# Moving SBUF tiles by 64 to 192 bytes in a two-layer float32 backbone on Trainium2

## The chip, the cores and the metric

The kernel runs on one core of one Trainium2 chip. The metric is the device time of one execution, in microseconds: 3413.97 us, the median of three runs (3413.45 to 3414.4). The engines are named as the profile names them: PE (TensorE, matmuls), PEld (its weight loads), DVE (VectorE), ACT (ScalarE), POOL (GpSimd) and SP (SyncE, which here issues loads).

## What is computed

The reference runs two layers over 1,024 latent tokens of 1,024 features and 256 context tokens, in float32. Cut to its shape:

```python
for l in range(DEPTH):                              # 2 layers
    shift, scale, gate = _ada(c, w_ada[l], b_ada[l])
    h_lat = _rms(x, norm_w[l]) * (1.0 + scale) + shift
    if l % 2 == 0:   # 16 heads of neighbourhood attention || 4 heads of two-way mLSTM
        y_lat, y_ctx = _ab_mixer(h_lat, h_ctx, w_in_ab[j], ...)
    else:            # 16 heads of two-way HGRN2 (gated linear recurrence)
        y_lat, y_ctx = _c_mixer(h_lat, h_ctx, w_in_c[j], ...)
    x = x + gate * y_lat
```

Each mixer is an input projection of the normalised tokens, the heads' own work, and an output projection.

## The kernel before

**Projections.** Float32 accuracy is had from three matmuls in the faster float32r type: each operand is split into a high and a low part (`split`, lines 71 to 75; ACT casts the high part, DVE subtracts for the low one), and `dense` (lines 127 to 133) issues high x high, high x low and low x high for each block of 128 features. The profile calls these lines 130, 131 and 132; lines 861 to 863 of `out_sum` are the same trio for the output projections. In every matmul one operand is the weights loaded into the array ahead of it (128 columns), the other is streamed (the moving operand, 256 or 512 columns). Which of the two is the token tile and which the weight matrix differs: `proj_nat` streams the weight matrix (`wh`, `wl`, `wzh`, `wzl`, `wxh`) against the tokens, `proj_tr` streams the tokens (`hh`, `hl`) against the weight matrix. The profile writes the output, then the moving tile, then the weights: `mm<-wh,hh` has `wh` moving.

**Stages.** After the normalisation come layer 0's attention heads (pool `na`), its mLSTM heads (pool `ml`), its output projection (pools `oy`, `op0`, `wo1`), then layer 1's sixteen recurrent heads (pool `hg`), and its output projection. In a recurrent head, `hg_proj` projects the gates, `hg_intra` works through seven levels inside blocks of tokens with strips of 64 columns (line 1024, plain float32), `hg_vz` projects the values and the gate (weights `wz`, moving in most of its matmuls), `hg_ctx` and `hg_scan` carry the state, and `hg_out` transposes and stores.

**Order and places.** The tile framework writes out each engine's order by a simulated timeline, and sets the waits. SBUF has two sides: pools opened on the left are stacked upwards from the constants (pool `const`), pools opened on the right are stacked downwards from the top. A pool's tiles lie one behind the other in the order in which their names first come up, each name with as many buffers as it asks for. So a tile that is added moves everything that was placed behind it, also in pools stacked on top. On the right lie `hh` and `hl` (the tokens' two parts), `w1` (layer 1's weight tiles) and `oy`. On the left lies the rest: the constants, `w0` (layer 0's weight tiles), `na`, `ml`, `pre`, `gates`, `op0`, `op1`, `wo1`, `hgk` and `hg`.

The lines that the change touches: `na_qk`, line 663 (the sums of squares `ar`, three buffers); `hg_vz`, line 939; `hg_intra`, line 994; `hg_scan`, line 1115 (the sums `gss`); `build`, where the constants are loaded, line 1207 on, and where the heads are called, line 1385.

Of the kernel before, what the change touches and what calls it, by code (L numbers as in the profile page):

```python
# [10 lines left out]
F32 = mybir.dt.float32  # L11
# [8 lines left out]
P = 128  # L20
# [25 lines left out]
class Prog:  # L46
# [599 lines left out]
    def na_qk(self, p2, pool):  # L646
        nc, a = self.nc, self.a
        w = self.wring([a["wab"][:, p2 * P : (p2 + 1) * P], a["wab"][:, D + p2 * P : D + (p2 + 1) * P]], 256)
        qs = [self.t(pool, [P, T], F32R, "aqs", 4) for _ in range(2)]
        kh = [self.t(pool, [P, T], F32R, "akh", 4) for _ in range(2)]  # L650
        kl = [self.t(pool, [P, T], F32R, "akl", 4) for _ in range(2)]

        for tt in range(0, NT, 2):
            ps = self.ps("mm", [P, 2, 256])
            for j in range(2):
                self.proj_nat(ps[:, j, :], w, tt + j, 0, 256)
            raw = self.t(self.wp, [P, 2, 256], F32, "ev", 2)
            nc.scalar.copy(raw, ps)
            n = self.t(pool, [P, 2, 2, P], F32, "aqn", 2)
            g = lambda t: t.rearrange("p a b -> p (a b)").rearrange("p (a b) -> p a b", b=64)  # L660
            n8 = n.rearrange("p a b c -> p (a b c)").rearrange("p (a b) -> p a b", b=64)
            nc.scalar.activation(n8, g(raw), AF.Square)
            r = self.t(pool, [P, 8], F32, "ar", 3)
            nc.vector.tensor_reduce(r, n8, axis=AX.X, op=ALU.add)
            self.rsqrt(r, r, 1.0 / 64)
            nc.vector.tensor_tensor(out=n8, in0=g(raw), in1=r.unsqueeze(2).to_broadcast([P, 8, 64]), op=ALU.mult)

            pt = self.ps("tq", [P, 4, P])
            for i in range(4):
                nc.tensor.transpose(pt[:, i, :], n[:, i % 2, i // 2, :], self.ident)  # L670
            pq = pt[:, 0:2, :].rearrange("p a b -> p (a b)")
            pk = pt[:, 2:4, :].rearrange("p a b -> p (a b)")
            s = slice(tt * P, (tt + 2) * P)
            for hd in range(2):
                own, oth = slice(hd * 64, (hd + 1) * 64), slice((1 - hd) * 64, (2 - hd) * 64)
                if tt < LAT // P:

                    qv = qs[hd][:, (tt // 4) * 512 : (tt // 4 + 1) * 512].rearrange("p (b r c) -> p r b c", b=4, r=8)
                    qv = qv[:, 2 * (tt % 4) : 2 * (tt % 4) + 4]
                    pv = pq.rearrange("p (r b c) -> p r b c", r=4, b=4)  # L680
                else:
                    qv, pv = qs[hd][:, s], pq

                nc.scalar.copy(qv[own], pv[own])
                nc.vector.tensor_tensor(out=qv[oth], in0=pv[own], in1=qv[own].bitcast(F32), op=ALU.subtract)
                for h64 in (own, oth):
                    nc.scalar.activation(kh[hd][h64, s], pk[own], AF.Copy, scale=self.qkn[own])
                    nc.vector.scalar_tensor_tensor(
                        out=kl[hd][h64, s], in0=pk[own], scalar=self.qkn[own], in1=kh[hd][own, s].bitcast(F32),
                        op0=ALU.mult, op1=ALU.subtract,  # L690
                    )
        return qs, kh, kl
# [246 lines left out]
    def hg_vz(self, h, st, pool):  # L939
        nc, a = self.nc, self.a  # L940
        col = lambda i: a["wc"][:, i * 2048 + h * P : i * 2048 + (h + 1) * P]
        w = self.wblock(pool, "wz", [col(3), col(4)], KD, 256)
        v = self.t(pool, [P, NT, P], F32, "gv", 2)
        z = self.t(pool, [P, NT - 2, P], F32, "gz", 1)
        ps = self.ps("mm", [P, CTX])
        self.proj_tr(ps, w, 0, LAT, CTX)
        vT = self.t(pool, [P, CTX], F32, "gEc", 1)
        nc.scalar.copy(vT, ps)  # L948
        pt = self.ps("tr", [P, 2, P])
        for j in range(2):  # L950
            nc.tensor.transpose(pt[:, j, :], vT[:, j * P : (j + 1) * P], self.ident)
        nc.scalar.copy(v[:, 8:10, :], pt)
        for tt in range(0, 8, 2):

            ps = self.ps("mm", [P, 2, 256])
            for j in range(2):
                self.proj_nat(ps[:, j, :], w, tt + j, 0, 256)
            nc.scalar.copy(v[:, tt : tt + 2, :], ps[:, :, 0:P])
            sg = self.t(pool, [P, 2, P], F32, "gsg", 1)
            nc.scalar.activation(sg, ps[:, :, P:256], AF.Sigmoid)  # L960
            nc.vector.tensor_tensor(out=z[:, tt : tt + 2, :], in0=sg, in1=ps[:, :, P:256], op=ALU.mult)
        st["v"], st["z"] = v, z
# [28 lines left out]
        return S  # L991


    def hg_intra(self, st, pool):
        nc = self.nc
        F, q = st["F"], st["q"]
        K = self.t(pool, [P, 2, LAT], F32, "gK", 1)
        nc.vector.tensor_scalar(out=K, in0=F, scalar1=-1.0, scalar2=1.0, op0=ALU.mult, op1=ALU.add)
        Q = self.t(pool, [P, 2, LAT], F32, "gQ", 1)
        ks = [self.t(pool, [P, 512], F32, "gkn", 4) for _ in range(2)]  # L1000
        for hf in (1, 0):
            s = slice(hf * 512, (hf + 1) * 512)
            nc.vector.tensor_tensor(out=ks[hf], in0=K[:, 0, s], in1=K[:, 1, s], op=ALU.add)
            for d in range(2):
                nc.vector.tensor_tensor(out=Q[:, 1 - d, s], in0=q[hf], in1=F[:, d, s], op=ALU.mult)
        hv = dict(Q=Q, K=K, T=F, D=self.t(pool, [P, 8, 64], F32, "gD", 1))
        hv["A"] = self.t(pool, [P, 8, P], F32, "gA", 1)
        pa = self.ps("s", [P, 8, 64])
        with self.urgent():
            for c in range(8):  # L1010
                for b in range(2):
                    o = c % 4 * P + b * 64
                    self.strip(pa[:, c, :], b, ks[c // 4][:, o : o + 64], q[c // 4][:, o : o + 64])
        nc.vector.tensor_tensor(
            out=hv["D"], in0=pa, in1=self.lmask[:, 0, :].unsqueeze(1).to_broadcast([P, 8, 64]), op=ALU.mult
        )
        for lev in range(7):
            self.hg_level(hv, lev, pool)
        return hv
# [64 lines left out]
    def hg_scan(self, st, H, S, pool):  # L1084
# [12 lines left out]
        for c in range(8):  # L1097
            cs = slice(c * P, (c + 1) * P)
            if c % 4 == 0:
                o4 = self.ps("acc", [P, 4, P])  # L1100
            o = o4[:, c % 4, :]
            nc.tensor.matmul(o, lhsT=H["A"][:, c, :], rhs=v[:, c, :], start=True, stop=False)  # L1102
            nc.tensor.matmul(o, lhsT=H["Q"][:, 0, cs], rhs=sb[c], start=False, stop=False)  # L1103
            nc.tensor.matmul(o, lhsT=H["Q"][:, 1, cs], rhs=Sf, start=False, stop=True)
            if c < 7:
                u = self.ps("s", [P, P])
                nc.tensor.matmul(u, lhsT=H["kn"][c // 4][0][:, c % 4, :], rhs=v[:, c, :], start=True, stop=True)
                s = self.t(pool, [P, P], F32, "gS0", 2)
                nc.vector.scalar_tensor_tensor(
                    out=s, in0=Sf, scalar=H["T"][:, 0, c : c + 1], in1=u, op0=ALU.mult, op1=ALU.add  # L1110
                )
                Sf = s
            if c % 4 < 3:
                continue
            ss = self.t(pool, [P, 4], F32, "gss", 2)
            jk = self.t(pool, [P, P], F32, "gjk", 1)
            for i in range(4):
                nc.scalar.activation(jk, o4[:, i, :], AF.Square, accum_out=ss[:, i : i + 1])
            self.rsqrt(ss, ss, 1.0 / P)

            y4 = H["A"][:, c - 3 : c + 1, :]
            nc.vector.tensor_tensor(out=y4, in0=o4, in1=z[:, c - 3 : c + 1, :], op=ALU.mult)
            nc.gpsimd.tensor_tensor(out=y4, in0=y4, in1=ss.unsqueeze(2).to_broadcast([P, 4, P]), op=ALU.mult)
# [51 lines left out]
    def build(self):  # L1175
        tc, nc, a = self.tc, self.nc, self.a
        dma = nc.sync.dma_start
        with ExitStack() as es:
# [23 lines left out]
            def load(name, shape, eng=nc.gpsimd):  # L1202
                t = self.t(cp, shape, F32, name)
                eng.dma_start(out=t, in_=a[name])
                return t

            self.sc = load("cT", [P, KD, 2], nc.sync)
            self.normw = load("normw", [P, 2, KD])
            self.badap = load("badap", [P, 2, 16])
# [84 lines left out]
            with tc.tile_pool(name="ml", bufs=2) as pool, self.pp.phase(s=2, acc=2):  # L1294
# [9 lines left out]
                st, parts = self.ml_load(0, pool)  # L1304
# [72 lines left out]
            with l1:  # L1377
# [4 lines left out]
                last = None  # L1382
                st = self.hg_proj(0, pool, wf)
                for h in range(16):
                    hv = self.hg_intra(st, pool)
                    self.hg_vz(h, st, pool)
                    self.hg_close(hv, pool)
                    S = self.hg_ctx(st, pool)
# [283 lines left out]
```

## Time and profile before

| what | value |
|---|---|
| runs | 3413.97 us median, 3413.45 to 3414.4 |
| profiled execution, its own time | 3411.4 us |
| its span, first to last instruction | 3409.6 us |
| granted PE clock, mean | 0.994 |
| instructions | 64360 |
| DMA, mean over the span | 100 GB/s |

The profile is one execution, so its rows add up to its own span and not to the median of the runs; the two are 2.6 us apart. A row's mean duration of a matmul covers its way through the array as well and is longer than the distance from one start to the next, since matmuls are pipelined: where matmuls follow each other without a gap, that distance is read from the start times in the timeline (start, duration, engine, line, operation, tiles, shape, count). Rows of grouped instructions give busy time and the mean of one, then the idle time ahead of them and what ended it. Rows of stretches give for each engine busy time and count, then the clock, the share of DMA, and GB/s.

### The profile page before, as it was taken

How to read it: one execution, taken by the hardware profiler on the slowest of the kernel's cores; microseconds unless marked ns; L12 is line 12 of the kernel's file. 1: busy time of each engine (PE TensorE's matmuls, PEld its weight loads, DVE VectorE, ACT ScalarE, POOL GpSimd, SP SyncE). 2: the span in 40 equal slices, each digit the busy share in tenths (PEclk: the TensorE clock that was granted, in tenths of full speed). 3: DMA queues.
4: the chain of work that ended last, by engine and by line, in shares of the span. 5: the costliest groups of instructions: out<-in, count | busy, mean ns of one | idle time of the engine just before them, and what ended most of it. 6: DMA issues, size and time to landing. Idle time of an engine off the chain costs nothing.

```text
span 3409.6 us, 64360 instructions
## 1 busy us (share of the span) xinstructions
PE 3353.0 (98%) x25044; PEld 2967.1 (87%) x25044; DVE 2019.0 (59%) x4772; ACT 1401.5 (41%) x3307; POOL 666.3 (20%) x1064
## 2 busy tenths in 40 slices
PE   7999999999999999999999999999999999999998
PEld 5689999889989888898888999988999999989877
DVE  5336666666655566687656555555555555555655
ACT  5335554455443444454454333333333333333343
POOL 2122222122211112221100121121121212222111
PEclk8999999999999999999999999999999999999999
DMA  6622222232233434444653122121222222222366
GB/s 247 212 77 71 75 81 73 81 91 76 73 88 103 141 116 126 134 129 141 208 173 94 46 66 69 57 66 63 66 64 68 78 60 61 62 75 72 81 178 169
DMA packets 327665, 341.69 MB, mean 100 GB/s; under 512 B 31209, under 2 KB 273577, under 8 KB 325313
## 3 DMA queue, kind: packets, MB, share of 16 engines
q1 hardware_dynamic: 280768, 216.21, 21.8%
q0 software_dynamic: 46592, 121.38, 11.5%
q8 instruction: 197, 3.23, 0.4%
q14 instruction: 108, 0.88, 0.1%
HBM read 252.84 MB, written 84.47 MB: 99 GB/s over the span
## 4 chain that ended last, share of the span: by engine, by line
PE 88%; issue 4%; DMA 3%; DVE 2%; POOL 1%; ACT 1%; SPq 0%; POOLq 0%; DVEq 0%; ACTq 0%
PE mm L130 19%; PE mm L132 19%; PE mm L131 19%; PE s L1024 4%; PE acc L799 2%; PE tr L779 2%; PE mm L861 2%; PE mm L863 2%; PE mm L862 2%; PE acc L571 2%; PE s L580 2%; PE acc L561 1%; PE acc L1102 1%; PE tr L1036 1%; PE acc L1103 1%
## 5 line engine op out<-in xcount | busy, mean ns | idle before, releaser
L132 PE MATMUL mm<-hh,wl 128*128 128x512 f32 (+1 forms) x1600 | 583.7, 365 | 0.0
L130 PE MATMUL mm<-hh,wh 128*128 128x512 f32 (+1 forms) x1600 | 583.6, 365 | 0.0
L131 PE MATMUL mm<-hl,wh 128*128 128x512 f32 (+1 forms) x1600 | 583.1, 364 | 0.0
L130 PE MATMUL mm<-wh,hh 128*128 128x256 f32 (+1 forms) x1520 | 473.6, 312 | 2.4 <-ACT ev L315 1.0
L132 PE MATMUL mm<-wh,hl 128*128 128x256 f32 (+1 forms) x1520 | 470.4, 310 | 0.3 <-DVE hl L274 0.3
L131 PE MATMUL mm<-wl,hh 128*128 128x256 f32 (+1 forms) x1520 | 470.5, 310 | 0.0
L132 PEld LDWEIGHTS mm<-hh,wl 128*128 128x128 f32 x1600 | 301.7, 189 | 44.9 <-issue 0.3
L130 PEld LDWEIGHTS mm<-hh,wh 128*128 128x128 f32 x1600 | 301.9, 189 | 44.3 <-ACT wh L73 0.8
L131 PEld LDWEIGHTS mm<-hl,wh 128*128 128x128 f32 x1600 | 301.8, 189 | 43.3 <-issue 0.2
L130 PEld LDWEIGHTS mm<-wh,hh 128*128 128x128 f32 x1520 | 286.9, 189 | 23.3 <-ACT ev L296 4.2
L132 PEld LDWEIGHTS mm<-wh,hl 128*128 128x128 f32 x1520 | 286.6, 189 | 12.9 <-issue 1.4
L131 PEld LDWEIGHTS mm<-wl,hh 128*128 128x128 f32 x1520 | 287.0, 189 | 12.3 <-issue 1.2
L130 PE MATMUL mm<-wzh,hh 128*128 128x256 f32 x1024 | 294.3, 287 | 0.2 <-ACT gEc L948 0.2
L132 PE MATMUL mm<-wzh,hl 128*128 128x256 f32 x1024 | 291.9, 285 | 0.0
L131 PE MATMUL mm<-wzl,hh 128*128 128x256 f32 x1024 | 290.3, 283 | 0.0
L74 DVE TENSOR_TENSOR wl<-wraw,wh 128x512 fp32r<-128x512 f32 x244 | 169.7, 700 | 181.1 <-ACT wh L73 177.3
L73 ACT CAST wh<-wraw 128x512 fp32r<-128x512 f32 x244 | 150.1, 619 | 250.6 <-PE mm L131 172.8
L130 PEld LDWEIGHTS mm<-wzh,hh 128*128 128x128 f32 x1024 | 192.5, 188 | 3.4 <-ACT gEc L948 0.6
L131 PEld LDWEIGHTS mm<-wzl,hh 128*128 128x128 f32 x1024 | 192.5, 188 | 1.4
L132 PEld LDWEIGHTS mm<-wzh,hl 128*128 128x128 f32 x1024 | 192.5, 188 | 1.2
L1054 ACT COPY gksel<-gK 128x1024 f32<-128x1024 f32 x96 | 111.0, 1156 | 180.6 <-PE s L1024 128.5
L1071 DVE TENSOR_TENSOR gQ<-gQ,gF 128x1024 f32<-128x1024 f32 x112 | 139.2, 1243 | 54.1 <-PE s L1024 53.4
(426 smaller groups left out, 7333.4 us busy)
## 6 DMA issues: line engine op xcount, KB each, us to landing
wraw<-in_wab_dram SPq DMA_DIRECT2D x112, 256.0 KB
wraw<-in_wc_dram SPq DMA_DIRECT2D x96, 256.0 KB
wraw<-yd SPq DMA_DIRECT2D x90, 256.0 KB
wraw<-in_wc_dram SPq DMA_DIRECT2D x128, 128.0 KB
md<-ev POOLq DMA_DIRECT2D x60, 256.0 KB, 2.8
mloz<-md SPq DMA_DIRECT2D x40, 256.0 KB
s<-gyt POOLq DMA_DIRECT2D x36, 256.0 KB, 4.2
adar<-in_wada_dram SPq DMA_DIRECT2D x8, 1024.0 KB
```

The costliest lines, as they stand in the source:

```text
L73: m = nc.scalar.copy(hi, x)
L74: nc.vector.tensor_tensor(out=lo, in0=x, in1=hi.bitcast(F32), op=ALU.subtract)
L130: mm(ps, lhsT=lh(k), rhs=rh(k), start=(start and k == 0), stop=False)
L131: mm(ps, lhsT=lh(k), rhs=rl(k), start=False, stop=False)
L132: m = mm(ps, lhsT=ll(k), rhs=rh(k), start=False, stop=(stop and k == nk - 1))
L571: nc.tensor.matmul(num, lhsT=qc[:, j, :], rhs=C[d][:, j, :], start=False, stop=(j == 1))
L580: nc.tensor.matmul(u, lhsT=st["k"][c][:, j * P : (j + 1) * P], rhs=vw, start=True, stop=True)
L779: nc.tensor.transpose(pt[:nk, i, :], pr[:, o : o + nk], self.ident)
L799: m = nc.tensor.matmul(yp[h64], lhsT=v[:, h64], rhs=pTs[hd][:nk, i, :], start=(i == turn[0]), stop=(i == turn[-1]), tile_position=(0, hd * ...
L1024: self.nc.tensor.matmul(out[s], lhsT=lhsT, rhs=rhs, start=True, stop=True, tile_position=(0, b * 64))
L1054: m = nc.scalar.copy(ksel.rearrange("p (b s i) -> p b s i", s=2, i=h), pick(K))
L1071: nc.vector.tensor_tensor(out=v, in0=v, in1=tot, op=ALU.mult)
```

## The change

Five edits, none of which adds an instruction that runs: a tile of 64 bytes is placed among the constants, ahead of the conditioning vector; a tile of 64 bytes is placed in the heads' pool, in the first head, behind `gA` and ahead of `gksel`; the two tiles of root sums `gss` are taken at the start of `hg_vz`, ahead of the values `gv`, and handed on, where they were taken in `hg_scan`; `ar` gets four buffers of 32 bytes where it had three; and `hg_intra` is told the head's number.

```diff
@@ na_qk
-            r = self.t(pool, [P, 8], F32, "ar", 3)
+            r = self.t(pool, [P, 8], F32, "ar", 4)
@@ hg_vz
         w = self.wblock(pool, "wz", [col(3), col(4)], KD, 256)
+        st["ss"] = [self.t(pool, [P, 4], F32, "gss", 2) for _ in range(2)]
         v = self.t(pool, [P, NT, P], F32, "gv", 2)
@@ hg_intra
-    def hg_intra(self, st, pool):
+    def hg_intra(self, h, st, pool):
...
         hv["A"] = self.t(pool, [P, 8, P], F32, "gA", 1)
+        if h == 0:
+            self.t(pool, [P, 16], F32, "pad", 1)
         pa = self.ps("s", [P, 8, 64])
@@ hg_scan
-            ss = self.t(pool, [P, 4], F32, "gss", 2)
+            ss = st["ss"][c // 4]
@@ build
+            self.t(cp, [P, 16], F32, "pad")
             self.sc = load("cT", [P, KD, 2], nc.sync)
...
-                    hv = self.hg_intra(st, pool)
+                    hv = self.hg_intra(h, st, pool)
```

In the two built programs the instructions, their order on each engine and their waits are the same, one for one. The start addresses in SBUF differ. Modulo 256 bytes they are:

| tiles | pool | before | after |
|---|---|---|---|
| `hh`, `hl` (tokens), both layers | right | 192 | 192 |
| `wh`, `wl` in layer 1; `woh`, `wol`, `yh`, `yl` of `oy` | right | 192 | 192 |
| `wh`, `wl` in layer 0 | `w0` | 64 | 128 |
| `wxh`, `wxl` | `gates` / `ml` | 128 / 64 | 192 / 128 |
| `aqs`, `akh`, `akl` | `na` | 64 | 128 |
| `az` to `arb` (behind `ar`) | `na` | 32 bytes more than the rest of the pool's shift | |
| `yh`, `yl`, `wraw` | `op0` | 192 | 0 |
| `woh`, `wol` at the very end | `wo1` | 0 | 64 |
| `wraw`, `gq`, `gK`, `gQ`, `gkn`, `gD`, `gA` | `hg` | 192 | 0 |
| `gksel`, `gT` | `hg` | 192 | 64 |
| `wzh`, `wzl` | `hg` | 0 | 128 |
| `gv`, `gz`, `gEc`, `gknc`, `gS0`, `gS1` | `hg` | 0 | 192 |

## The prediction

> **What bounds the kernel now.** First the page: the busy shares and the tenths by slice.
>
> ```profile
> PE 3353.0 (98%) x25044; PEld 2967.1 (87%) x25044; DVE 2019.0 (59%) x4772; ACT 1401.5 (41%) x3307; POOL 666.3 (20%) x1064
> ...
> PE   7999999999999999999999999999999999999998
> ...
> PEclk8999999999999999999999999999999999999999
> ...
> PE 88%; issue 4%; DMA 3%; DVE 2%; POOL 1%; ACT 1%; SPq 0%; POOLq 0%; DVEq 0%; ACTq 0%
> ```
>
> PE is busy in every slice, the clock is granted in full, and the chain that ended last is 88% PE. Next, the busy time by stretches, one in the attention stage (layer 0) and one in the recurrent heads (layer 1).
>
> ```profile
> 340.00:510.00 170.00, 170.00 (x1375) 155.36 (x1374) 113.60 (x359) 87.82 (x239) 42.88 (x58) 1.00 0.27 77
> 2040.00:2210.00 170.00, 170.00 (x1516) 154.27 (x1515) 94.56 (x152) 57.99 (x119) 30.71 (x46) 1.00 0.19 58
> ```
>
> PE is busy 170 us of 170 in both, at clock 1.00, and no other engine is above 114. So the time of these stages is the number of matmuls times the distance from one start to the next (the pitch). Only what changes a pitch changes the time there. Nothing else can: in the two built programs every engine has the same instructions in the same order with the same waits; only SBUF addresses differ.
>
> **Which operations feel an address.** ScalarE first, where one line casts tiles that start at different residues (all residues here are start addresses modulo 256): wh from 64 to 64 or 192 to 192, wzh from 192 to 0.
>
> ```profile
> L73 ACT CAST wh<-wraw 128x512 fp32r<-128x512 f32 x244 | 150.1, 619 | 250.6 <-PE mm L131 172.8 <-DMA wraw<-in_wab_dram 48.4 <-DVE og L897 11.7
> ...
> L73 ACT CAST wzh<-wraw 128x512 fp32r<-128x512 f32 x64 | 39.7, 620 | 64.8 <-DMA wraw<-in_wc_dram 64.5
> ...
> L498 PE MATMUL s<-mqT,mkT 128*128 128x128 f32 x160 | 23.3, 275 | 0.0
> ...
> L987 PE MATMUL s<-gv,gknc 128*128 128x128 f32 x128 | 16.8, 274 | 0.0
> ```
>
> 619 and 620 ns: no effect. The last two are plain float32 matmuls of 128 columns, pairs (moving 64, weights 64) and (0, 0): 275 and 274 ns, no effect. The float32r matmuls of 512 and 256 columns are another matter. I read their pitch from the timeline: first and last row of an unbroken run. In a name the moving tile stands first, then the weights. First 512 columns.
>
> ```profile
> 1838.25 0.40 PE L130 MATMUL mm<-hh,wh 128*128 128x512 f32 x1
> ...
> 1865.25 0.39 PE L132 MATMUL mm<-hh,wl 128*128 128x512 f32 x1
> ...
> 425.78 0.40 PE L131 MATMUL mm<-hl,wh 128*128 128x512 f32 x1
> ...
> 431.13 0.40 PE L130 MATMUL mm<-hh,wh 128*128 128x512 f32 x1
> ...
> 1143.18 0.39 PE L131 MATMUL mm<-wl,hh 128*128 128x512 f32 x1
> ...
> 1147.59 0.40 PE L132 MATMUL mm<-wh,hl 128*128 128x512 f32 x1
> ...
> 1574.36 0.39 PE L861 MATMUL mm<-wh,wxh 128*128 128x512 f32 x1
> ...
> 1576.17 0.39 PE L863 MATMUL mm<-wh,wxl 128*128 128x512 f32 x1
> ...
> 3324.00 0.41 PE L130 MATMUL c<-woh,yh 128*128 128x512 f32 x1
> ...
> 3398.65 0.39 PE L863 MATMUL mm<-woh,yl 128*128 128x512 f32 x1
> ...
> 107.52 0.39 PE L130 MATMUL mm<-wxh,hh 128*128 128x512 f32 x1
> ...
> 108.68 0.39 PE L132 MATMUL mm<-wxh,hl 128*128 128x512 f32 x1
> ```
>
> In this order: (192, 192), 120 matmuls, 27.00/119 = 226.9 ns. (192, 64), 24 matmuls, 5.35/23 = 232.6. (64, 192), 20 matmuls, 4.41/19 = 232.1. (64, 64), 9 matmuls in layer 0, 1.81/8 = 226.3. (0, 192), 327 matmuls, 74.65/326 = 229.0. (128, 192), 6 matmuls, 1.16/5 = 232.0, a run too short to have settled. The fourth pair matters most: it lies in layer 0, where all other pitches are near 232, so residues and not the stage make the difference. Equal residues give 227, a distance of 128 gives 232, a distance of 64 gives 229 or 232.
>
> Now 256 columns.
>
> ```profile
> 250.04 0.29 PE L130 MATMUL mm<-wh,hh 128*128 128x256 f32 x1
> ...
> 258.82 0.28 PE L132 MATMUL mm<-wh,hl 128*128 128x256 f32 x1
> ...
> 243.53 0.28 PE L130 MATMUL mm<-hh,wh 128*128 128x256 f32 x1
> ...
> 246.29 0.28 PE L132 MATMUL mm<-hh,wl 128*128 128x256 f32 x1
> ...
> 1969.87 0.28 PE L130 MATMUL mm<-wzh,hh 128*128 128x256 f32 x1
> ...
> 1973.88 0.28 PE L131 MATMUL mm<-wzl,hh 128*128 128x256 f32 x1
> ...
> 1865.48 0.28 PE L130 MATMUL mm<-hh,wzh 128*128 128x256 f32 x1
> ...
> 1868.19 0.28 PE L132 MATMUL mm<-hh,wzl 128*128 128x256 f32 x1
> ...
> 2383.82 0.28 PE L131 MATMUL mm<-hl,wzh 128*128 128x256 f32 x1
> ...
> 2385.64 0.28 PE L132 MATMUL mm<-hh,wzl 128*128 128x256 f32 x1
> ...
> 2160.29 0.28 PE L130 MATMUL mm<-hh,wh 128*128 128x256 f32 x1
> ...
> 2163.04 0.28 PE L132 MATMUL mm<-hh,wl 128*128 128x256 f32 x1
> ```
>
> (64, 192), 75 matmuls, 8.78/74 = 118.6 ns. (192, 64), 24, 2.76/23 = 120.0. (0, 192), 35, 4.01/34 = 117.9. (192, 0), 24, 2.71/23 = 117.8; the same pair in a later head, 17, 1.82/16 = 113.8. (192, 192), 24, 2.75/23 = 119.6. Here a distance of 64 is the best, equal the worst, and the pair (192, 0) has two rhythms, 117.8 and 113.8, whichever it falls into after the work ahead of it.
>
> The Trainium skill, "TensorE: Matmul & The Clock Gate", section "Step-by-step: what each phase is for", says that TensorE reads the moving operand and the weights through two independent ports, so that loading weights takes nothing from a running matmul. By that rule every term below is zero. The pairs at 226.3 and 232.1 ns, of equal size and in one layer, speak against it.
>
> **The change part by part.** The counts of matmuls by pair are from the built programs; the two largest groups stand on the page, once for each of lines 130 to 132:
>
> ```profile
> L130 PE MATMUL mm<-wh,hh 128*128 128x256 f32 x1280 | 373.3, 292 | 1.7 <-ACT ev L315 1.0 <-ACT hh L273 0.6
> ...
> L130 PE MATMUL mm<-wzh,hh 128*128 128x256 f32 x1024 | 294.3, 287 | 0.2 <-ACT gEc L948 0.2
> ```
>
> The pad among the constants moves layer 0's weight tiles from 64 to 128; hh and hl stay at 192.
> - 3,840 matmuls of 256 columns, weight tiles moving against hh: (64, 192) to (128, 192), a pair that no run of that width shows. It comes to distance 64; nearest are 117.9 and 117.8. I take 117.8: 3,840 x -0.8 ns = **-3.1 us**. Ends: 113.8 (-18.4) and 120.0 (+5.4).
> - 600 of 256 columns, hh moving: (192, 64) to (192, 128), also distance 64. Other runs of this pair are shorter and nearer 119, so I take -1.5 ns: **-0.9 us**; ends -3.7 and 0.
> - 1,206 of 512 columns, mostly hh moving: (192, 64) to (192, 128). The shift from moving to weights is then that of (0, 192), 229.0: 1,206 x -3.6 = **-4.3 us**; ends -6.9 (226.9) and 0.
> - 1,062 of 512 columns, weight tiles moving: (64, 192) to (128, 192). The short run says 232.0, the mirrored distance 229.0. I take half: 1,062 x -1.6 = **-1.7 us**; ends -5.5 and 0.
>
> The 64 bytes in the heads' pool, placed behind gA in head 0, and the pad together move wz by 128.
> - 3,072 of 256 columns, wz moving: (0, 192) to (128, 192). Distance 64 before and after: **0**; ends 113.8 (-12.6) and 120.0 (+6.5).
> - 384 of 256 columns with wz as weights: (192, 0) to (192, 128): 0; ends 0 and +1.5, when the faster rhythm is lost.
> - 336 of 512 columns at the end: (0, 192) to (64, 192): 336 x +3.1 = **+1.0 us**. Two small groups (84 and 60) cancel.
> - The strips of line 1024 go from (192, 192) to (0, 64), and to (0, 0) in two levels' worth; gv, gS against gkn, gA, gQ from (0, 192) to (192, 0). All are plain float32, for which the rows above show no effect. I take 0. The strips are 64 wide, though, and no such pair is seen at other residues:
>
> ```profile
> L1024 PE MATMUL s<-gQ,gksel 128*64 128x64 f32 x3072 | 118.3, 231 | 7.1 <-DVE gQ L1005 7.1
> ```
>
> 118.3 us busy; a 5% shift, the spread between the 256-column pitches (113.8 to 120.0), is 6 us either way.
>
> The root sums (gss) ahead of the values move gv to 192 and add no instruction. The fourth buffer of ar could let a later sum start before an earlier one is read, but the built programs have the same waits, so it only moves az to arb by 32 bytes more: 0. DMA targets move too; PE waits for no transfer in the stretches above, and where it is not covered (the first and last slices) I allow 1 us either way.
>
> Sum: -3.1 - 0.9 - 4.3 - 1.7 + 1.0 = **-9.0 us**. PE is busy without a gap where the terms lie, so it passes through whole; what comes next late are the evictions by ACT, busy 88 of 170 us, far from a limit. The profiled execution took 3411.4 us (span 3409.6) and would take 3402.4. The median of the runs is 3414.0, so I forecast 3405.0.
>
> **The rivals.**
> - *Nothing happens*: the pitch is not set by these residues, or the new pairs stay at 232 and 118.6. For it: the only run of (128, 192), at 232.0. Against it: 226.3 beside 232.1 in layer 0. Time 3414. The port rule of the Trainium skill, quoted above from "TensorE: Matmul & The Clock Gate", "Step-by-step: what each phase is for", would give the same time.
> - *The faster rhythm*: (128, 192) has the same shift of weights against moving tile as (192, 0), which ran at 113.8 in a later head. If half of the 3,840 and the 3,072 fall into it, another 0.5 x (3,840 x 4.0 + 3,072 x 4.1) = 14 us go: 3391. Against it: the first head stayed at 117.8 for all its 24.
> - *Slower*: wide and narrow need not agree, as equal residues show (best at 512, worst at 256). If (128, 192) is a bad pair at 256 columns, with the 120.0 of (192, 64), it costs +5.4 and +6.5, +0.8 for the 384 that fall from 117.8 to 120.0, +1.0 at the end, with no gain at 512: +13.7, so 3428 (3422 if the 512-column gains still come). It decides from a rise of 0.9 ns over the 6,912 moving weight tiles (5.9 us, what the other terms give together).
> - *The change does not do what it says* (it also moves waits): excluded by the equal programs.
>
> **How the numbers follow.** Forecast 0.42, nothing 0.20, faster rhythm 0.22, slower 0.16. About 0.2%, 6.8 us, can be told from no change. Around -9.0 the forecast lies beyond that bound in four of five cases: faster 0.34 + 0.22 = 0.56, same 0.08 + 0.20 = 0.28, slower 0.16. The range goes from 3388, past the half-way rhythm, to 3421, half of the way to the slower case: it leaves out part of these two, under 0.2 together.
>
> **What would show it.** Equal counts and orders of matmuls; hh against wh at 512 columns in layer 0 falling from 232.6 to near 229; wh against hh at 256 from 118.6 to near 117.8; wz against hh unchanged at 117.9; hh against layer 1's w at 226.9 and 119.6, whose addresses stay; all ACT and DVE rows within 1%. The forecast is wrong if the 256-column rows go to 113.8 (too cautious) or 120 (wrong sign), if the strips of line 1024 move, or if the gain in layer 0 turns up as idle time before PE.

## The result and the profile after

The changed kernel takes 3395.77 us (median of six runs, 3391.8 to 3397.98); the kernel before took 3414.18 us beside it (six runs, 3412.36 to 3417.18). The ratio is 0.9943, 95% interval 0.9930 to 0.9955: faster by 0.57%. The profiled execution took 3395.39 us with a span of 3393.6 us, 16.0 us less than the 3409.6 before, at the same mean clock (0.994).

The page of the changed kernel, busy shares and the chain that ended last; then its stretches, as shown of before:

```profile
PE 3334.6 (98%) x25044; PEld 2950.6 (87%) x25044; DVE 2018.8 (59%) x4772; ACT 1401.4 (41%) x3307; POOL 665.4 (20%) x1064
...
PE 86%; issue 5%; DMA 4%; DVE 2%; POOL 1%; ACT 1%; SPq 0%; POOLq 0%; DVEq 0%; ACTq 0%
```

```profile
340.00:510.00 170.00, 170.00 (x1368) 155.37 (x1367) 115.12 (x365) 89.70 (x243) 42.89 (x58) 1.00 0.28 79
2040.00:2210.00 170.00, 169.94 (x1503) 154.26 (x1502) 92.54 (x149) 55.20 (x111) 31.50 (x49) 1.00 0.21 68
```

DVE, ACT and POOL are busy for as long as before, to within 1 us. PE's busy time falls by 18.4 us (3353.0 to 3334.6), and PE still has next to no idle time in either stretch (0.06 us): there each matmul comes sooner. Over the whole span PE's idle time (span less busy time) is 2.4 us longer than before, 59.0 for 56.6 us. (The counts of a stretch can't be compared, since the work that lies in it has moved.)

The same groups as before, by line and shape (busy time, mean ns of one):

```profile
L130 PE MATMUL mm<-wh,hh 128*128 128x256 f32 x1280 | 369.8, 289 | 2.0 <-ACT hh L273 1.1 <-ACT ev L315 1.0
...
L130 PE MATMUL mm<-wzh,hh 128*128 128x256 f32 x1024 | 294.3, 287 | 0.8 <-ACT gEc L949 0.7
...
L1027 PE MATMUL s<-gQ,gksel 128*64 128x64 f32 x3072 | 117.5, 230 | 7.6 <-DVE gQ L1006 7.6
```

The first was 373.3 us and 292 ns, the second the same as here, though its pitch falls (below), the strips (then line 1024) 118.3 us and 231 ns. A mean of one contains the way through the array; the pitch is in the starts. First and last row of seven unbroken runs, from the timeline of the changed kernel:

```profile
216.21 0.28 PE L132 MATMUL mm<-wh,hl 128*128 128x256 f32 x1
224.37 0.28 PE L132 MATMUL mm<-wh,hl 128*128 128x256 f32 x1
...
245.83 0.28 PE L132 MATMUL mm<-wh,hl 128*128 128x256 f32 x1
247.60 0.28 PE L132 MATMUL mm<-wh,hl 128*128 128x256 f32 x1
...
1871.54 0.28 PE L131 MATMUL mm<-wzl,hh 128*128 128x256 f32 x1
1874.03 0.28 PE L132 MATMUL mm<-wzh,hl 128*128 128x256 f32 x1
...
2030.92 0.28 PE L131 MATMUL mm<-wzl,hh 128*128 128x256 f32 x1
2035.04 0.28 PE L130 MATMUL mm<-wzh,hh 128*128 128x256 f32 x1
...
178.35 0.39 PE L132 MATMUL mm<-hh,wl 128*128 128x512 f32 x1
187.28 0.39 PE L132 MATMUL mm<-hh,wl 128*128 128x512 f32 x1
...
1131.47 0.39 PE L132 MATMUL mm<-wh,hl 128*128 128x512 f32 x1
1136.13 0.40 PE L132 MATMUL mm<-wh,hl 128*128 128x512 f32 x1
...
3309.19 0.40 PE L132 MATMUL c<-woh,yl 128*128 128x512 f32 x1
3382.39 0.40 PE L863 MATMUL mm<-woh,yl 128*128 128x512 f32 x1
```

`wh` against the tokens, 256 columns: 73 matmuls, 8.16/72 = 113.3 ns, and another run of 16 at 1.77/15 = 118. `wz`, 256 columns: 23 at 2.49/22 = 113.2, and 36 at 4.12/35 = 117.7. So the pair (128, 192) has the two rhythms that the pair (192, 0) had before. At 512 columns: tokens against `wh` 40 at 8.93/39 = 229.0 (before 232.6); `wh` against tokens 21 at 4.66/20 = 233.0 (before 232.1); the last projection 316 at 73.20/315 = 232.4 (before 229.0).

What each term came to: the two programs issue the same 25044 matmuls in one order, so each distance from one start to the next can be set beside the same one before (gap for gap, as it is called from here on). The pitch is the mean inside the unbroken runs of a group. The us are the sum of all differences of up to 20 ns behind a matmul of the group, and they count the breaks between runs too, which shrink less. (Some counts are a little below the prediction's, since the names in a trace don't tell every pool apart.)

| term (moving, weights) | count | pitch before, after (ns) | us | forecast |
|---|---|---|---|---|
| 256, `w0` tiles moving | 3,840 | 118.8, 115.4 | -11.4 | -3.1 |
| 256, `wz` moving | 3,072 | 117.6, 115.6 | -5.5 | 0 |
| 512, tokens moving, layer 0 | 1,200 | 232.7, 229.9 | -3.2 | -4.3 |
| 512, `w0` and `wx` tiles moving | 960 | 232.5, 233.0 | +0.7 | -1.7 |
| 256, tokens moving against `w0` | 576 | 118.8, 116.9 | -1.1 | -0.9 |
| 256, tokens moving against `wz` | 384 | 115.3, 117.4 | +0.6 | 0 |
| 512, last projection | 336 | 229.0, 232.4 | +1.1 | +1.0 |
| plain float32 of 64 columns (the strips) | 4,096 | | -0.8 | 0 |
| all other groups | | | +0.4 | 0 |

They add up to -19.1 us (before rounding). Another 106 distances differ by more than 20 ns, because PE waits there, or runs at half clock (granted 0.51 from 1566.1 to 1573.0 us before, 0.50 from 3003.8 to 3007.2 us after); they add 2.6 us and leave the 16.0 us of the span to within 0.5. In a second execution of the changed kernel (span 3391.3 us) the pitches give -18.8 us and the rest nothing: the pitches are the change's, the waits are those of one execution.

### The profile page after: what moved, and what is told of

Same layout as the page of the kernel before. It is cut to its first block, busy times and chain, and to the rows that moved or that the text cites. A ratio compares the mean times of both kernels' runs of the same rounds, so it can differ in the third digit from the quotient of the medians.

```text
span 3393.6 us, 64360 instructions
## 1 busy us (share of the span) xinstructions
PE 3334.6 (98%) x25044; PEld 2950.6 (87%) x25044; DVE 2018.8 (59%) x4772; ACT 1401.4 (41%) x3307; POOL 665.4 (20%) x1064
## 4 chain that ended last, share of the span: by engine, by line
PE 86%; issue 5%; DMA 4%; DVE 2%; POOL 1%; ACT 1%; SPq 0%; POOLq 0%; DVEq 0%; ACTq 0%
PE mm L130 19%; PE mm L132 19%; PE mm L131 19%; PE s L1027 4%; PE acc L799 2%; PE tr L779 2%; PE mm L861 2%; PE mm L863 2%; PE mm L862 2%; PE acc L571 2%; PE s L580 2%; PE acc L561 1%; PE acc L1105 1%; PE tr L1039 1%; PE acc L1106 1%
## 5 line engine op out<-in xcount | busy, mean ns | idle before, releaser
L130 PE MATMUL mm<-wzh,hh 128*128 128x256 f32 x1024 | 294.3, 287 | 0.8 <-ACT gEc L949 0.7
```

What stands on the lines that cost most here:

```text
L130: mm(ps, lhsT=lh(k), rhs=rh(k), start=(start and k == 0), stop=False)
```

## What the traces suggest, and the rivals

Write d for the start of the weights minus the start of the moving tile, modulo 256 bytes. Sorted by d, with its sign kept, the two traces fall into one table: 512 columns 227 to 229 ns at d = 0, 233 at 64, 232 at 128, 229 to 230 at 192; 256 columns 119 to 120 at 0, 113 or 118 at 64, 119 at 128, mostly 118 at 192. **Theory:** d alone sets the pitch, or the pair of rhythms (steady pitches) that it can have. **Rivals:** the residue of one tile by itself counts; each pad has a gain of its own, so that the parts add up; the other two edits (`gss`, `ar`) do some of it; any move would have done.

## The experiments

**The pairs by themselves.** A kernel that only issues matmuls, each with its own weight load, one d after the other.

```diff
+        def run(w, o, m, r, n, count):
+            for k in range(count // 3):
+                mm(ps[:, :n], lhsT=a(k), rhs=h(k), start=True, stop=True)
+                mm(ps[:, :n], lhsT=a(k), rhs=l(k), start=True, stop=True)
+                mm(ps[:, :n], lhsT=b(k), rhs=h(k), start=True, stop=True)
```

> Leaves the reference's work out: it only issues matmuls, each with its own weight load, in the order in which the kernel's projections issue them, in runs of 96 of one pair of start residues; the moving tile's name gives the distance d = (weights start - moving start) mod 256 bytes (d064 with weights wt at 0), bf16 tiles are named b, and plain float32 runs use the tile src. Theory (distance alone sets the pitch): float32r of 512 columns d=0 226.9 ns, d=64 233, d=128 232.3, d=192 229.5; of 256 columns d=0 119.7, d=64 113.3 or 117.8 depending on how the run starts, d=128 119, d=192 117.3; the same values within 1 ns when the weights start at 64 (tile wu) instead of 0. Rival (absolute residues or the surrounding work set it): wu and wt differ by 3 ns or more at one d, or all d agree within 1 ns here because no other engine works. Plain float32 of 128 and 64 columns: within 1% at all d by both. For the steps between (16, 32, 48, 80, 96, 160, 224) and for bf16 neither theory has a number; if only the 64-byte line counts, 16 to 48 equal d=0 or d=64.

Its timeline; the profile drops the digits of a tile's name, so the runs are told by their order. First and last of 49 matmuls each: 512 columns at d = 0, 64 and 192; 256 columns at d = 64, 128 and 192; and d = 192 with the weights at 64. Then bf16 of 256 columns at d = 0 and 64 (a whole run in one row), and plain float32 at several d (566 rows of the trace in one; a plain float32 matmul has two, here called passes).

```profile
27.85 0.39 PE L56 MATMUL acc<-d,wt 128*128 128x512 f32 x1
38.73 0.39 PE L56 MATMUL acc<-d,wt 128*128 128x512 f32 x1
...
119.02 0.40 PE L56 MATMUL acc<-d,wt 128*128 128x512 f32 x1
130.22 0.40 PE L56 MATMUL acc<-d,wt 128*128 128x512 f32 x1
...
233.06 0.39 PE L56 MATMUL acc<-d,wt 128*128 128x512 f32 x1
244.04 0.39 PE L56 MATMUL acc<-d,wt 128*128 128x512 f32 x1
...
320.24 0.28 PE L56 MATMUL acc<-d,wt 128*128 128x256 f32 x1
325.68 0.28 PE L56 MATMUL acc<-d,wt 128*128 128x256 f32 x1
...
355.53 0.28 PE L56 MATMUL acc<-d,wt 128*128 128x256 f32 x1
361.23 0.28 PE L56 MATMUL acc<-d,wt 128*128 128x256 f32 x1
...
379.10 0.28 PE L56 MATMUL acc<-d,wt 128*128 128x256 f32 x1
384.54 0.28 PE L56 MATMUL acc<-d,wt 128*128 128x256 f32 x1
...
527.69 0.28 PE L56 MATMUL acc<-d,wu 128*128 128x256 f32 x1
533.34 0.28 PE L56 MATMUL acc<-d,wu 128*128 128x256 f32 x1
...
599.75 63.31 PE L79 MATMUL acc<-src 128*128 128x128 f32 x566
...
748.06 10.64 PE L87 MATMUL acc<-b,w 128*128 128x256 bf16 x96
...
758.99 10.64 PE L87 MATMUL acc<-b,w 128*128 128x256 bf16 x96
```

By 48 steps: 226.7, 233.3 and 228.8 ns; 113.3, 118.8, 113.3, and 117.7. The mean over the second half of each run, where it has settled:

| d | 0 | 16 | 32 | 48 | 64 | 80 | 96 | 128 | 160 | 192 | 224 |
|---|---|---|---|---|---|---|---|---|---|---|---|
| 512, weights at 0 | 226.7 | 233.3 | 233.3 | 234.7 | 233.3 | 233.3 | 234.3 | 232.4 | 233.3 | 228.9 | 233.3 |
| 512, weights at 64 | 226.7 | | | | 233.3 | | | 232.4 | | 228.9 | |
| 256, weights at 0 | 120.0 | 117.1 | 118.3 | 119.1 | 113.3 | 119.2 | 118.7 | 118.7 | 120.0 | 113.3 | 116.7 |
| 256, weights at 64 | 120.0 | | | | 113.3 | | | 118.6 | | 117.8 | |

No other engine works here, and the pitches are those of the kernel; where both weights' starts were tried they agree within 0.2 ns at each d, but for d = 192 at 256 columns, which ran once at 113.3 and once at 117.8. So d counts, and steps of 16 bytes count too: from d = 0 to 16 the pitch goes from 226.7 to 233.3 ns at 512 columns and from 120.0 to 117.1 at 256, and at 16 to 48 no value is as good as the best at the multiples of 64. Behind other work, d = 64 at 256 columns went into 113.3 in four of eight runs and into 117.8 in the other four, and always into 117.8 behind 512 columns at d = 0. Of the types and widths tried, only float32r feels d: bf16 of 256 columns takes 10.64 us for 96 at each of four d (109.2 ns from start to start), and plain float32 of 128 and 64 columns 111.7 ns a pass, from start to start, at each of four d (63.31 us for 566, the last one's way through the array included).

**The constants' pad alone.**

```diff
+            self.t(cp, [P, 16], F32, "pad")
             self.sc = load("cT", [P, KD, 2], nc.sync)
```

> Kernel before with the 64 bytes among the constants alone; layer 0's weight tiles go from 64 to 128, the heads' wz from 0 to 64. Distance theory: layer 0 as in the whole change (256-column 3,840 matmuls -11.1 us, 512-column token-moving -3.1, 600 of 256 -1.2, the rest about 0), but wz against hh goes from distance 192 to 128 (117.6 to 118.9 ns, 3,072 times +1.3 = +4.0 us), hh against wz from 64 to 128 (+1.4), the last output projection +2.1: -8 us in all, 3406, ratio 0.9977. Rival (parts add up, each with its own gain): layer 0's -15 us stay and wz does not matter: ratio 0.9955 or lower.

Measured: 3402.05 us, ratio 0.9976 (0.9967 to 0.9986). Groups of this kernel, `wh` and `wz` against the tokens:

```profile
L130 PE MATMUL mm<-wh,hh 128*128 128x256 f32 x1280 | 369.8, 289 | 1.9 <-ACT ev L315 1.0 <-ACT hh L273 0.9
...
L130 PE MATMUL mm<-wzh,hh 128*128 128x256 f32 x1024 | 296.2, 289 | 0.1
```

Layer 0 has all it has in the whole change (369.8 us there too), but `wz` got slower, 294.3 to 296.2 us. The parts do not add up by themselves.

**The heads' part alone.**

```diff
+        st["ss"] = [self.t(pool, [P, 4], F32, "gss", 2) for _ in range(2)]
...
+        if h == 0:
+            self.t(pool, [P, 16], F32, "pad", 1)
```

> Kernel before with the heads' part alone (64 bytes behind gA, gss ahead of gv): wz goes from 0 to 64, nothing else that feeds float32r matmuls moves. Distance theory: slower, wz against hh from distance 192 to 128, +4.0 us, hh against wz from 64 to 128, +1.4 us: +5.4 us, 3419.5, ratio 1.0016. Rival (the heads' pad has a gain of its own, the -3.3 us of wz seen with the whole change): ratio 0.999 or lower. Rival (nothing but chance): 1.000.

Measured: 3414.47 us, ratio 1.0005 (0.9996 to 1.0014). The group of `wz`:

```profile
L130 PE MATMUL mm<-wzh,hh 128*128 128x256 f32 x1024 | 295.9, 289 | 0.0
```

The pitch of `wz` went from 117.6 to 118.4 and that of the tokens against it from 115.3 to 118.6, as d says; gap for gap that is +2.4 and +1.2 us. The medians show +2.3 us (the kernel before took 3412.17 us beside it). The expected ratio, 1.0016, lies just above the interval, which holds no change as well, but no gain as large as the rival's. Each pad alone leaves `wz` at d = 128; only both together bring it to 64.

**The other side moved.** The left tiles stay; the tokens, `w1` and `oy` go down by 64.

```diff
-            nc.vector.memset(self.t(edge, [P, 8], F32, "edge"), 0.0)
+            nc.vector.memset(self.t(edge, [P, 24], F32, "edge"), 0.0)
```

> Kernel before with 64 bytes more in the tile at the right edge: hh, hl, w1 and oy go down by 64, from 192 to 128; every tile on the left stays. By distance this is the same as the constants' pad alone: w0 against hh 64, hh against w0 192, wz against hh 128. Distance theory: layer 0's 256-column pitch from 118.9 to about 115.8, 512-column token-moving from 232.5 to 229.8; wz against hh up to 118.9; -8 us in all, ratio 0.9977, as the constants' pad alone. Rival (absolute residues of the left tiles set the pitch, so that w0 at 128 is what helped): layer 0 keeps 118.9 and 232.5 ns, ratio 1.000 or higher.

Measured: 3403.75 us, ratio 0.9975 (0.9966 to 0.9985).

```profile
L130 PE MATMUL mm<-wh,hh 128*128 128x256 f32 x1280 | 369.8, 289 | 2.4 <-ACT hh L273 1.3 <-ACT ev L315 1.0
...
L130 PE MATMUL mm<-wzh,hh 128*128 128x256 f32 x1024 | 296.9, 290 | 0.0
```

Other tiles at other addresses, and the same times as with the constants' pad. A residue by itself does not count.

**Both sides moved.**

```diff
+            nc.vector.memset(self.t(edge, [P, 24], F32, "edge"), 0.0)
...
-            mx = self.t(cp, [P, 16], F32, "lbm")
+            mx = sg.rearrange("p a b -> p (a b)")
```

> Kernel before with everything moved down by 64 bytes, on the right by a wider tile at the edge, on the left by one constant of 64 bytes taken out (a scratch tile is shared). Every start residue of a float32r tile changes, no distance does. Distance theory: every pitch as in the kernel before (118.9, 117.7, 232.6, 232.3, 116 ns), ratio 1.000 within 0.0015. Rival (absolute residues count, or any move of the tiles helps): layer 0's pitches move by a nanosecond or more and the ratio is off 1.000 by 0.002 or more.

Measured: 3413.18 us, ratio 1.000 (0.9991 to 1.0008).

```profile
L130 PE MATMUL mm<-wh,hh 128*128 128x256 f32 x1280 | 374.2, 292 | 1.6 <-ACT ev L315 1.0 <-ACT hh L273 0.6
```

Every float32r tile has a new residue and no d is new: nothing happens. Gap for gap, this group's pitch rose by 0.1 ns, and those of the other groups in the table of terms moved by 0.2 ns at most.

**The other two edits alone.**

```diff
+            r = self.t(pool, [P, 8], F32, "ar", 4)
...
+        st["ss"] = [self.t(pool, [P, 4], F32, "gss", 2) for _ in range(2)]
```

> Kernel before with gss ahead of gv and the fourth buffer of ar alone, no pad: gv, gz, gEc, gknc and gS move by 64 bytes, az to arb by 32; no float32r tile of the projections moves. Distance theory: ratio 1.000 within 0.001, the strips and all ACT and DVE rows within 1%. Rival (these two edits carry part of the gain by themselves): ratio 0.998 or lower.

Measured: 3411.31 us, ratio 0.9995 (0.9986 to 1.0004); gap for gap, the pitches of layer 0's large groups are within 0.1 ns of before and that of `wz` 0.4 ns below it, and the strips have a median duration of 222 ns, as before and after. No gain of the rival's size is there. One group moved, though its addresses did not, the last projection; its first and last row:

```profile
3323.12 0.40 PE L132 MATMUL c<-woh,yl 128*128 128x512 f32 x1
3396.62 0.39 PE L863 MATMUL mm<-woh,yl 128*128 128x512 f32 x1
```

316 matmuls, 73.50/315 = 233.3 ns, where the same pair (0, 192) took 229.0 in the kernel before. So at d = 192 the 512 columns, too, have more than one rhythm: d sets which ones a pair has, not always which one it takes.

**Equal residues in layer 0** (d = 0).

```diff
+            self.t(cp, [P, 32], F32, "pad")
```

> Kernel before with 128 bytes among the constants, gss ahead of gv and the fourth buffer of ar, no pad in the heads: layer 0's weight tiles at 192 as hh (distance 0), wz at 128 (distance 64). Distance theory, by the pitches measured at distance 0 elsewhere: wh against hh of 256 columns 118.9 to 119.6 (3,840 times, +2.7 us), hh against wh of 512 columns 232.7 to 228.5 (1,152 times, -4.8), wh and wxh moving at 512 columns 232.3 to 228.2 (1,060 times, -4.3), wz 117.7 to 116.5 (-3.6), the small ones +2: -8 us in all, ratio 0.9977. Rival (the 256-column matmuls follow the 512-column ones, equal residues best for both): 256 columns at 116 or less, -11 us more, ratio 0.9945.

Measured: 3403.64 us, ratio 0.9970 (0.9959 to 0.9981).

```profile
L130 PE MATMUL mm<-wh,hh 128*128 128x256 f32 x1280 | 374.8, 293 | 1.7 <-ACT ev L315 1.0 <-ACT hh L273 0.7
```

`wh` against the tokens at 256 columns went from 118.8 to 119.5 ns, at 512 columns tokens moving from 232.7 to 228.8 and `wh` moving from 232.5 to 229.6: a loss at 256 and a gain at 512, as in the table. The largest part of this gain, though, is `wz`, which has d = 64 here: 117.6 to 114.8 ns, gap for gap -7.8 us where -3.6 was expected, with 47 of its 51 unbroken runs of 24 matmuls or more in the faster rhythm.

**Each distance at its best.**

```diff
+            self.t(mlk, [P, 16], F32, "pad")
...
+            self.t(pool, [P, 32], F32, "pad", 1)
...
+                self.t(pool, [P, 16], F32, "pad", 1)
...
+                self.t(wl1, [P, 48], F32, "pad")
```

> Every distance set to the best one seen: the 64 bytes only among layer 0's tiles (not among the constants), 128 bytes in the heads' pool, 64 ahead of the mLSTM stage's tiles, 192 ahead of the last output projection's weights. Distance theory against the whole change: last output projection 336 times 232.3 to 227.2 ns (-1.7 us), wxh of the mLSTM stage 180 times 233.1 to 229 (-0.7), the tiles against op0's y and gF 84 times 233 to 229 (-0.4): -2.8 us, ratio to before 0.9935 where the whole change has 0.9943. Rival (the end is hidden behind the last loads and stores): as the whole change, 0.9943.

Measured: 3391.18 us, ratio 0.9935 (0.9921 to 0.9948). First and last row of the last projection in its timeline:

```profile
3306.90 0.39 PE L132 MATMUL c<-woh,yl 128*128 128x512 f32 x1
3378.32 0.39 PE L863 MATMUL mm<-woh,yl 128*128 128x512 f32 x1
```

316 matmuls, 71.42/315 = 226.7 ns where the whole change has 232.4. It is the fastest version here, though its interval overlaps that of the whole change. Gap for gap against the whole change, the last projection gives 1.8 us, as expected. A further 2.5 us come from `wz`, whose d is 64 in both: here 49 of its 51 unbroken runs of 24 matmuls or more are in the faster rhythm, there 26. No term of the expectation had that.

**The changed kernel again**, with no edit, beside the kernels with both sides moved, with equal residues and with each distance at its best.

> The changed kernel once more, beside the three others on one chip. Both theories: ratio 0.9943 within 0.001.

Measured: 3393.76 us, ratio 0.9942 (0.9930 to 0.9955); the best version is 2.6 us below it, where 2.8 was expected. That the sum agrees is in part luck, since the rhythm of `wz` is in it.

**Which distance, and which rhythm.** Pairs in turn, and short runs behind other work.

```diff
+            for k in range(96):
+                one(k, k % 2 * 64, k % 2 * 64, n, (ma, mb)[k % 2])
...
+            for k in range(96):
+                one(k, k % 2 * 64, 64 - k % 2 * 64, n, (mb, ma)[k % 2])
```

> Leaves the reference's work out; it only issues matmuls, each with its own weight load. First, which distance counts: pairs of start residues taken in turn, 96 matmuls each, (moving 0, weights 0) with (64, 64), where the distance to the matmul's own weights is always 0 and to the weights loaded next 64 and 192 in turn; then (64, 0) with (0, 64), where the own distance is 192 and 64 and that to the next weights always 0. If the load of the next weights beside the stream is what collides: at 512 columns 231.2 ns (mean of 233.4 and 229.0) in the first and 226.7 in the second. If the own pair counts: 226.7 in the first and 231.2 in the second. If the address makes both equal, neither explains it. At 256 columns: by the next load 113.3 to 117.8 in the first and 120.0 in the second, by the own pair the reverse. Then runs of 24 of 256 columns at distance 64 (52 of them) and 192 (52), behind plain float32, 512-column and 256-column matmuls: if the distance alone decides the rhythm, one pitch for each distance; if the start decides, 113.3 and 117.8 both at both distances, with a larger share of 113.3 at 64 than at 192 (in the kernels about two thirds against one in twenty-five).

Its timeline, 49 matmuls each: own distance 0 at 512 columns, distance to the next weights 0 at 512; then the two at 256.

```profile
20.16 0.39 PE L46 MATMUL acc<-mb,wu 128*128 128x512 f32 x1
31.28 0.39 PE L46 MATMUL acc<-mb,wu 128*128 128x512 f32 x1
...
42.92 0.40 PE L46 MATMUL acc<-ma,wu 128*128 128x512 f32 x1
54.12 0.40 PE L46 MATMUL acc<-ma,wu 128*128 128x512 f32 x1
...
60.28 0.28 PE L46 MATMUL acc<-mb,wu 128*128 128x256 f32 x1
65.88 0.28 PE L46 MATMUL acc<-mb,wu 128*128 128x256 f32 x1
...
72.07 0.29 PE L46 MATMUL acc<-ma,wu 128*128 128x256 f32 x1
77.83 0.29 PE L46 MATMUL acc<-ma,wu 128*128 128x256 f32 x1
```

231.7, 233.3, 116.7 and 120.0 ns. A matmul's distance to its own weights alone is out: where it was 0, 512 columns did not get 226.7, nor 256 columns 120. Three of four values are those of the load of the next weights beside the stream; the second, 233.3 where 226.7 was expected, is not (233.3 is also the slower rhythm of the last projection above), and stays open. Of the 52 short runs at d = 64, 25 settled at 113.3 and 27 at 117.8; at d = 192, 2 and 50. What goes before weighs in: at d = 64 all eight runs behind 256 columns at d = 0 went to 113.3, all sixteen behind 512 columns at d = 0 or 192 to 117.8. Behind 1 to 12 plain float32 matmuls they went to 113.3 for 2, 3, 6, 7, 10 and 11, and to 117.8 for the rest. The count alone doesn't decide it: in the first experiment runs behind one such matmul settled at 113.3 twice and at 117.8 once.

## Why the prediction was right, and where it was not

**Right.** The time is 3395.8 us where 3405.0 was forecast (range 3388 to 3421), faster, and through pitches: ACT and DVE are as busy as before, and the strips fell by 0.7% (118.3 to 117.5 us), far from the 5% allowed for. That `gss` and `ar` cost nothing stands (0.9995). Four terms came within 1.1 us: tokens moving at 512 (-3.2 for -4.3) and at 256 against `w0` (-1.1 for -0.9), tokens against `wz` (+0.6 for 0), and the last projection (+1.1 for +1.0). The size was not right: the gain is about twice the 9.0 us forecast, and the time lies within the range because the range had room for the faster rhythm.

**The step that was mis-sized** is "nearest are 117.9 and 117.8. I take 117.8", for the 3,840 and, as "Distance 64 before and after", for the 3,072. It folded d = 64 and d = 192 into one distance. They differ: before, all 51 unbroken runs of 24 or more matmuls of `wz` (d = 192) settled at 117.8; after, at d = 64, 31 of 40 such runs of `w0` tiles and 26 of 51 of `wz` settled at 113.3. The row that said so was in the prediction: (192, 0), the one pair with the sign of (128, 192), had a rhythm of 113.8. That is -11.4 and -5.5 us instead of -3.1 and 0, and it is the sign that the prediction named for itself: "the 256-column rows go to 113.8 (too cautious)".

**The step that was wrong** is the half taken for the 512-column weight tiles: "The short run says 232.0, the mirrored distance 229.0". Mirrored is another d; the six matmuls of the short run were near the truth (233.0 after), and the term is +0.7 us instead of -1.7.

**The rivals.** "The faster rhythm" is what the two big groups did, nearly as it was priced: its 14 us beyond the forecast were 13.8. The time, 3395.8, lies between the forecast and its 3391, nearer to the rival, since the two large 512-column terms gave 3.5 us less than forecast. "Nothing happens" is excluded by the interval. So is what the prediction took from the port rule of the Trainium skill, "TensorE: Matmul & The Clock Gate", section "Step-by-step: what each phase is for". The bf16 runs agree with that rule (10.64 us at each d), the float32r runs don't (226.7 to 234.7 ns by d at 512 columns). The price of "slower", 120.0 ns at 256 columns, is that of d = 0, not of d = 64.

**Not settled:** why d counts at all, what makes a run fall into 113.3 or 117.8 at one d or the last projection into 229.0 or 233.3, and the second value of the last experiment. The choice of rhythm is hardly chance: in the second execution of the changed kernel, 89 of the 91 unbroken runs of 24 or more (`w0` tiles and `wz`) settled as in the first. So something in the program, in the work ahead of a run it seems, decides it, and no run here shows what.

## What to carry to other kernels

Where PE is busy without a gap on float32r matmuls that each load their weights, compare the two operands' start addresses modulo 256: equal starts were best at 512 columns (226.7 against up to 234.7 ns), weights 64 bytes past the moving tile at 256 columns (113.3 to 117.8 against 120.0). The distance has a sign, and a pad moves everything placed behind it, so judge a pad by all pairs that it changes, not by the one it is meant for. When a pair's pitch is read from a trace, read several runs of it: one run may show only one of two rhythms.

## What was not expected of the hardware

- The distance has a sign (at 512 columns 233.3 ns at d = 64, 228.9 at 192) and counts below 64 bytes (226.7 at d = 0, 233.3 already at 16).
- At 256 columns d = 64 and d = 192 have two stable rhythms, 113.3 and 117.8 ns, and at 512 columns d = 192 has 229.0 and 233.3; a run that has settled keeps its own (316 matmuls at 233.3).
- Of the types tried only float32r feels it: bf16 kept 109.2 ns at 256 columns at every d tried. The Trainium skill, "TensorE: Matmul & The Clock Gate", section "Back-to-back issue gap", gives N/2.4 + 2.5 ns for an isolated matmul at full clock, which for 256 columns comes to 109.2. These bf16 runs, with a weight load for each matmul, agree with it, and no float32r pair here reaches it.
